# Attention values over 64 weight columns with two heads side by side, a new split of the convolution taps, and four early output blocks in a two-layer encoder

## The chip, the cores and the metric

The kernel runs on one core of one Trainium2 chip. The metric is the device time of one execution in microseconds (us). Where the profile speaks of engines, PE is TensorE's matmul side, PEld its weight loads, DVE is VectorE, ACT is ScalarE, POOL is GpSimd and SP is SyncE, which issues most DMAs.

## The reference

Two layers of a Conformer-like block work on 512 tokens of 1024 features in float32. Each layer is a half-weighted SwiGLU, a mixing part, a second SwiGLU and a norm. The change lies in the mixing part alone, which runs two groups beside each other on the same projection: attention in 8 heads (queries and keys of 96 features, values of 64, block-causal by chunks of 64 tokens), and a causal depthwise convolution of 31 taps over 512 channels, with layer norm and swish. One projection takes both:

```python
h = rms_norm(x, mix_norm[l])
p = h @ w_in[l]
attn = mla_group(p[..., :o_kv], p[..., o_kv:o_pe], p[..., o_pe:o_cv], ...)
conv = conv_group(p[..., o_cv:], conv_w[l], conv_b[l], conv_ln_g[l], conv_ln_b[l])
x = x + jnp.concatenate([attn, conv], axis=-1) @ w_out[l]
...
probs = jax.nn.softmax(scores, axis=-1).astype(vs.dtype)
outs.append(jnp.einsum('bhqk,bhkd->bqhd', probs, vs))
...
y = lax.conv_general_dilated(u, conv_w[:, None, :], window_strides=(1,), padding=[(CONV_K - 1, 0)], ...)
return jax.nn.silu(layer_norm(y + conv_b, ln_g, ln_b))
```

## The kernel before, in words

Features lie on the 128 partitions and the 512 tokens along the free axis. Weight products are made from operands split into a high and a low part, three matmuls each (`mm3`, L154 to L156), with 512, 384, 288 or 256 moving columns. The products inside attention are plain float32 matmuls, and each of those stands as two instructions (each with its own weight load) in the trace.

`mix_body` first makes the projections in the order of `SEQ`: convolution group 0, the query latents, the gate of group 0, group 1, the key latents, the queries (`queries`), the keys (`keys`), then groups 2 and 3. In `queries` and `keys` each of the four token tiles ends in a power of -1/2 on POOL (`rsqrt`, L173), called `scq` for queries and `sck` for keys; DVE multiplies the keys by `sck` (L782 to L785), and only then does PE turn queries and keys of the first two heads (L811, L816).

Then the heads run staggered by `ORDER`: `turn` (transposes), `scores` (four blocks of 128 to 512 columns, L834, with the mask L835; DVE takes the maximum, L836; ACT the exponential, L840), `turn_p` (10 transposes of the probabilities, L855, copied by DVE and ACT, L858), `values` and `turn_out`. In `values` the turned probabilities are the 128 weight columns and 64 columns of V move, 10 matmuls a head (L868). When a pair of heads is done, DVE multiplies by the reciprocal sums (L875), PE turns the result back (L886), and `split` makes its high and low part (ACT L161, DVE L162).

The convolution has four groups of 128 channels and 31 taps, `CONV = "DAAD"`. In a group of kind D, DVE runs 30 multiply-adds into a PSUM bank (L922). In a group of kind A, ACT makes each tap's product into one of three `pr` buffers (L926) and POOL adds it (L930); from the 16th tap on, and in all of group 2 and later, those adds are issued behind the last `sck`. The four groups are summed by POOL (`ysum`, L944 to L946), PE takes the mean over channels (L948), DVE subtracts it (L954), ACT squares, PE sums the squares (L198), POOL takes the root, PE spreads it (L217), and scaling, swish and `split` (L964, L966, L161, L162) give the convolution half of the output projection. `early_groups` issues the attention half of the first output blocks (12 matmuls each) into that chain of small steps: `WOG = 3` blocks, two between L948 and L198, one between L198 and L217.

The scheduler fixes the order on each engine when the program is built, from program order, dependences, and `issue_after`, which holds an instruction behind another. Each engine then runs its list strictly in order.

Of the kernel before, what the change touches and what calls it, by code (L numbers as in the profile page):

```python
# [7 lines left out]
FP = mybir.dt.float32  # L8
# [4 lines left out]
ALU = mybir.AluOpType  # L13
# [61 lines left out]
def encoder_kernel(ctx: ExitStack, tc: tile.TileContext, xT, consts, vecs, rgain, wgu1, wd1, wdq1,  # L75
# [11 lines left out]
    def nm(s):  # L87
        uid[0] += 1
        return f"{s}{uid[0]}"
# [527 lines left out]
    def mix_body(kpool, l, gx, norm, done):  # L617
        u, order = [], {}

        def kept(dt=FP):  # L620
            return kpool.tile([P, S], dt, tag="m", name=nm("m"), bufs=2 * WIDE)
        ys = [None if kind == "D" else kpool.tile([P, S], FP, tag="y", name=nm("y"), bufs=2) for kind in CONV]

        def glu(pa, pg):
            tg = tmp()
# [40 lines left out]
        def latent_k():  # L666

            pk = [bank() for _ in range(NT)]
            for k0 in range(0, KD, 3):
                n = min(3, KD - k0)  # L670
                wh, wl = load_w(wkl[l, :, k0 * KW:(k0 + n) * KW], n * KW, "k")
                for k in range(k0, k0 + n):
                    cs = slice((k - k0) * KW, (k - k0 + 1) * KW)
                    for t in range(NT):
                        ts_ = slice(t * P, (t + 1) * P)
                        mm3(pk[t][:, :KW], gx[k][0][:, ts_], gx[k][1][:, ts_], wh[:, cs], wl[:, cs],
                            k == 0, k == KD - 1)
            for t in range(NT):
                A.copy(ckl[t // 2][:, t % 2], pk[t][:, :KVL])
                A.copy(cke[:, t], pk[t][:, KVL:KW])  # L680
                j = tmp()
                A.activation(j[:, :KVL], pk[t][:, :KVL], AF.Square, accum_out=ssl[:, t:t + 1])
                j = tmp()
                A.activation(j[:, :DR], pk[t][:, KVL:KW], AF.Square, accum_out=sspe[:, t:t + 1])


        tabs = []
# [173 lines left out]
        def values(h):  # L861

            if h % 2 == 0:
                heads[h]["po"] = bank()
            po = heads[h - h % 2]["po"].rearrange("p (t h d) -> p t h d", t=NT, h=2)
            for t in range(NT):
                for j in range(t + 1):
                    T.matmul(po[:, t, h % 2], heads[h]["pt"][j][:, (t - j) * P:(t - j + 1) * P],  # L868
                             vs[j][:, h * DV:(h + 1) * DV], start=j == 0, stop=j == t)
# [5 lines left out]
            V.tensor_tensor(o.rearrange("p (t h d) -> p t h d", t=NT, h=2), po,  # L875
                            rs[:, :, :, None].to_broadcast([P, NT, 2, DV]), ALU.mult)
            heads[h]["o"] = o

        def turn_out(h):

            if h % 2 == 0:
                return
            o = heads[h]["o"]
            ps = bank()
            for t in range(NT):
                T.transpose(ps[:, t * P:(t + 1) * P], o[:, t * P:(t + 1) * P], ident)  # L886
# [27 lines left out]
        for c in range(4):  # L914
            kind = CONV[c]
            acc = psum.tile([P, S], FP, tag="cv", name=nm("cv"), bufs=1) if kind == "D" else ys[c]
            tap = lambda k: cw[:, c * CK + k:c * CK + k + 1]
            A.activation(acc, u[c], AF.Identity, scale=tap(CK - 1), bias=cb[:, c:c + 1])  # L918
            for k in range(CK - 2, -1, -1):
                s = CK - 1 - k  # L920
                if kind == "D":
                    V.scalar_tensor_tensor(acc[:, s:], u[c][:, :S - s], tap(k), acc[:, s:], ALU.mult, ALU.add)  # L922
                    continue
                pr = kpool.tile([P, S], FP, tag="pr", name=nm("pr"), bufs=3)
                if kind == "A":
                    A.activation(pr[:, s:], u[c][:, :S - s], AF.Copy, scale=tap(k))  # L926
                else:
                    G.tensor_scalar(pr[:, s:], u[c][:, :S - s], tap(k), None, ALU.mult)
                with tc.issue_after(order["keys"]) if s >= PAUSE or c > 1 else nullcontext():
                    order["conv"] = G.tensor_tensor(acc[:, s:], acc[:, s:], pr[:, s:], ALU.add).ins  # L930
            if kind == "D":
                A.copy(u[c], acc)
                ys[c] = u[c]
        early = []

        def early_groups(ms):
# [11 lines left out]
        T.matmul(pm, onesm, ysum, start=True, stop=True)  # L948
        if PRELOAD:
# [291 lines left out]
```

## Time and profile before

| | us |
|---|---|
| three runs, median (lowest to highest) | 1799.76 (1798.87 to 1799.94) |
| the profiled execution | 1798.87 |
| its span, first to last instruction | 1797.1 |
| PE busy in the span | 1781.8 (99%) |
| DVE busy | 1494.5 (83%) |
| ACT busy | 1107.5 (62%) |
| POOL busy | 421.5 (23%) |

The span is divided into stages with different limits. The mixing part stands at about 350 to 560 us in layer 0 and 1240 to 1450 us in layer 1. POOL has almost all its work there. The granted TensorE clock is full in the whole execution. PE's ends are modelled, so a group of matmuls is best timed by its start and the start of what follows it.

### The profile page before, as it was taken

The page shows a single profiled execution, that of the slowest core. Times are in us where ns is not written, and L with a number is a line of the kernel's source. Part 1 is how long each engine was busy: PE and PEld are TensorE (multiplying, and loading weights), DVE is VectorE, ACT ScalarE, POOL GpSimd, SP SyncE. Part 2 cuts the span into 40 slices and gives each one's busy share as a digit, 9 for nine tenths or more (in the row PEclk, how much of TensorE's full clock was granted, in tenths as well). Part 3 has the DMA queues.
Part 4 walks back from the last instruction along what each step waited for, and adds up shares of the span by engine and source line. Part 5 has one row for each costly group of instructions (what it writes and reads, how often), then busy time and mean ns, then how long its engine had stood idle before and what let it go on. Part 6 is the DMA issues. An engine that isn't in the chain of part 4 may idle for free.

```text
span 1797.1 us, 29235 instructions
## 1 busy us (share of the span) xinstructions
PE 1781.8 (99%) x11334; PEld 1602.4 (89%) x11334; DVE 1494.5 (83%) x2299; ACT 1107.5 (62%) x1721; POOL 421.5 (23%) x343
## 2 busy tenths in 40 slices
PE   9999999999999999999999999999999999999998
PEld 7899999888788899999888999998978788999997
DVE  7898988589956989898779989876998668989883
ACT  5575756457953575756645757554779435756564
POOL 1000000258943000000310000002689410000002
PEclk9999999999999999999999999999999999999999
DMA  5657575325103466665426575743250125575742
GB/s 168 171 131 182 135 177 123 109 88 134 33 22 102 123 164 161 155 160 132 123 65 170 122 194 122 193 112 111 81 147 7 46 82 160 140 183 134 182 117 74
DMA packets 70413, 226.16 MB, mean 126 GB/s; under 512 B 7937, under 2 KB 8321, under 8 KB 70273
## 3 DMA queue, kind: packets, MB, share of 16 engines
q1 hardware_dynamic: 54000, 169.74, 30.3%
q0 software_dynamic: 16128, 54.53, 18.0%
q8 instruction: 89, 1.46, 0.3%
q14 instruction: 52, 0.42, 0.1%
q10 hardware_dynamic: 144, 0.00, 0.0%
HBM read 222.15 MB, written 2.10 MB: 125 GB/s over the span
## 4 chain that ended last, share of the span: by engine, by line
PE 91%; ACT 3%; DVE 2%; POOL 2%; issue 1%; DMA 0%; SPq 0%; ACTq 0%; POOLq 0%; DVEq 0%
PE ps L154 24%; PE ps L156 23%; PE ps L155 23%; PE ps L373 11%; PE ps L374 6%; PE ps L868 1%; PE ps L834 1%; POOL y L930 1%; ACT pr L926 1%; ACT r L840 1%; PE ps L855 1%; PE ps L198 0%; POOL sck L173 0%; PE ps L217 0%; DVE wl L246 0%
## 5 line engine op out<-in xcount | busy, mean ns | idle before, releaser
L155 PE MATMUL ps<-r,wh 128*128 128x256 f32 (+1 forms) x2540 | 806.8, 318 | 0.0
L154 PE MATMUL ps<-r,wh 128*128 128x256 f32 (+1 forms) x2540 | 803.6, 320 | 2.2 <-ACT wh L138 0.7
L156 PE MATMUL ps<-r,wl 128*128 128x256 f32 (+1 forms) x2348 | 749.2, 321 | 0.0
L154 PEld LDWEIGHTS ps<-r,wh 128*128 128x128 f32 x2540 | 480.5, 189 | 47.0 <-ACT wh L138 3.6
L155 PEld LDWEIGHTS ps<-r,wh 128*128 128x128 f32 x2540 | 481.6, 190 | 35.8 <-DVE r L162 1.5
L156 PEld LDWEIGHTS ps<-r,wl 128*128 128x128 f32 x2348 | 445.1, 190 | 33.5 <-DVE wl L144 0.4
L373 PE MATMUL ps<-xj,wh 128*128 128x512 f32 x864 | 303.9, 392 | 0.0
L138 ACT CAST wh<-raw 128x1024 fp32r<-128x1024 f32 (+3 forms) x148 | 131.9, 899 | 208.1 <-PE ps L155 125.8
L390 POOL DMA_DIRECT2D ls<-in_wgu x72 | 62.7, 871 | 734.7 <-ACT ls L389 595.3
L244 ACT CAST wh<-fr 128x1024 fp32r<-128x1024 f32 (+1 forms) x160 | 157.6, 985 | 104.4 <-DVE fr L410 53.2
L144 DVE TENSOR_TENSOR wl<-raw,wh 128x1024 fp32r<-128x1024 f32 (+3 forms) x132 | 145.3, 1108 | 91.3 <-ACT wh L138 90.9
L246 DVE TENSOR_TENSOR wl<-fr,wh 128x1024 fp32r<-128x1024 f32 (+1 forms) x160 | 182.3, 1139 | 20.3 <-ACT wh L244 20.3
L373 PEld LDWEIGHTS ps<-xj,wh 128*128 128x128 f32 x864 | 161.4, 188 | 30.1
L930 POOL TENSOR_TENSOR y<-y,pr 128x511 f32<-128x511 f32 (+14 forms) x120 | 158.6, 1322 | 54.5 <-ACT pr L926 47.1
L374 PE MATMUL ps<-xj,ls 128*128 128x256 f32 x576 | 161.3, 280 | 0.0
L244 ACT CAST wh<-raw 128x1024 fp32r<-128x1024 f32 (+1 forms) x100 | 98.2, 982 | 45.1 <-PE ps L155 24.2
L246 DVE TENSOR_TENSOR wl<-raw,wh 128x1024 fp32r<-128x1024 f32 (+1 forms) x100 | 113.5, 1135 | 14.2 <-ACT wh L244 13.7
L191 POOL TENSOR_TENSOR r<-r,t 128x512 f32<-128x512 f32 x45 | 75.0, 1676 | 175.6 <-ACT t L187 174.8
L374 PEld LDWEIGHTS ps<-xj,ls 128*128 128x128 f32 x576 | 108.3, 188 | 0.0
L389 ACT ACTIVATE ls<-fr 128x1024 fp32r<-128x1024 f32 (+1 forms) x56 | 56.1, 1002 | 74.5 <-PE ps L374 42.8
L926 ACT ACTIVATE pr<-m,vec 128x511 f32<-128x511 f32 (+14 forms) x120 | 85.7, 736 | 13.2 <-POOL y L930 13.2
L922 DVE SCALAR_TENSOR_TENSOR cv<-m,vec,cv 128x511 f32<-128x511 f32 (+14 forms) x120 | 87.8, 732 | 3.6 <-ACT cv L918 2.2
(241 smaller groups left out, 2944.9 us busy)
## 6 DMA issues: line engine op xcount, KB each, us to landing
fr<-in_wgu SPq DMA_DIRECT2D x112, 512.0 KB, 4.2
ls<-in_wgu POOLq DMA_DIRECT2D x72, 512.0 KB, 6.2
raw<-in_wgu SPq DMA_DIRECT2D x62, 512.0 KB, 4.5
fr<-in_wdq SPq DMA_DIRECT2D x48, 384.0 KB, 4.6
ls<-in_wdq POOLq DMA_DIRECT2D x32, 384.0 KB, 4.8
raw<-in_wd SPq DMA_DIRECT2D x32, 384.0 KB, 3.2
raw<-in_wd SPq DMA_DIRECT2D x32, 256.0 KB, 2.8
raw<-in_wcv SPq DMA_DIRECT2D x16, 512.0 KB, 3.6
```

Source lines behind the costliest of these rows:

```text
L138: order["cast"] = A.copy(hi[:, :w], raw[:, :w]).ins
L144: (G if kind in POOLW.split() else V).tensor_tensor(lo[:, :w], raw[:, :w], hi[:, :w].bitcast(FP), ALU.subtract)
L154: T.matmul(o, lh, rh, start=first, stop=False, skip_group_check=free)
L155: T.matmul(o, lh, rl, start=False, stop=False, skip_group_check=free)
L156: order["mm"] = T.matmul(o, ll, rh, start=False, stop=last, skip_group_check=free).ins
L244: A.copy(hi[:, :w], src[:, :w])
L246: order["lo"] = V.tensor_tensor(lo[:, :w], src[:, :w], hi[:, :w].bitcast(FP), ALU.subtract).ins
L373: T.matmul(o, w[0][:, c], both, start=start and k == 0, stop=False, skip_group_check=True)
L374: last = T.matmul(o[:, 0:HS], w[1][:, c], both[:, 0:HS], start=False, stop=k == 3, skip_group_check=True).ins
L922: V.scalar_tensor_tensor(acc[:, s:], u[c][:, :S - s], tap(k), acc[:, s:], ALU.mult, ALU.add)
L926: A.activation(pr[:, s:], u[c][:, :S - s], AF.Copy, scale=tap(k))
L930: order["conv"] = G.tensor_tensor(acc[:, s:], acc[:, s:], pr[:, s:], ALU.add).ins
```

## The change

Three things are altered, all in `mix_body`, and so twice in the program.

**Values.** For a pair of heads, V's 64 columns are the weights and the turned probabilities move (128 to 512 columns, 4 matmuls a head). The first head of a pair writes PSUM partitions 0 to 63, the second 64 to 127, in turns; each instruction carries a tile of 128 rows by 64 columns, at column 0 or 64. The result comes out already turned, so the four transposes of `turn_out` go. The reciprocal sums must now run along the free axis: 8 matmuls a pair spread them (a broadcast column as weights, the identity moving), and ACT copies the result to SBUF. DVE's multiplication reads that copy, and `split` reads SBUF instead of PSUM.

**Convolution.** `TAPS = (14, 20, 31, 0)` gives each group the number of taps that go by ACT and POOL; DVE makes the rest in PSUM and adds the two sums. Group 2 is all ACT and POOL, group 3 all DVE. From the fifth tap on, ACT's products of groups 1 and 2 are held behind the last square of the key latents. `ysum` is built by DVE as the groups end.

**Output.** `WOG = 4` and `E1 = 1`: one block's attention half is issued ahead of the mean, one between mean and squares, one between squares and spread, one behind.

```diff
-CONV = "DAAD"
+TAPS = (14, 20, 31, 0)
+HELD = 5
...
-E1 = 0
-YP = 1
+E1 = 1
 E2 = 2
 E3 = 3
-WOG = 3
+WOG = 4
...
-            return kpool.tile([P, S], dt, tag="m", name=nm("m"), bufs=2 * WIDE)
+            return kpool.tile([P, S], dt, tag="m", name=nm("m"), bufs=10)
...
         def values(h):
             if h % 2 == 0:
-                heads[h]["po"] = bank()
-            po = heads[h - h % 2]["po"].rearrange("p (t h d) -> p t h d", t=NT, h=2)
-            for t in range(NT):
-                for j in range(t + 1):
-                    T.matmul(po[:, t, h % 2], heads[h]["pt"][j][:, (t - j) * P:(t - j + 1) * P],
-                             vs[j][:, h * DV:(h + 1) * DV], start=j == 0, stop=j == t)
-            if h % 2 == 0:
                 return
             rs = small.tile([P, NT, 2], FP, tag="rs", name=nm("rs"))
             V.reciprocal(rs, heads[h - 1]["sums"])
+            pr = bank()
+            for t in range(NT):
+                for i in range(2):
+                    T.matmul(pr[i * DV:(i + 1) * DV, t * P:(t + 1) * P], rs[:, t, i:i + 1].to_broadcast([P, DV]),
+                             ident, start=True, stop=True)
+            r = tmp()
+            A.copy(r, pr)
+            po = bank()
+            for j in range(NT):
+                for i in range(2):
+                    T.matmul(po[i * DV:(i + 1) * DV, j * P:], vs[j][:, (h - 1 + i) * DV:(h + i) * DV],
+                             heads[h - 1 + i]["pt"][j], start=j == 0, stop=j == NT - 1)
             o = tmp()
-            V.tensor_tensor(o.rearrange("p (t h d) -> p t h d", t=NT, h=2), po,
-                            rs[:, :, :, None].to_broadcast([P, NT, 2, DV]), ALU.mult)
+            V.tensor_tensor(o, po, r, ALU.mult)
             heads[h]["o"] = o
...
-            o = heads[h]["o"]
-            ps = bank()
-            for t in range(NT):
-                T.transpose(ps[:, t * P:(t + 1) * P], o[:, t * P:(t + 1) * P], ident)
-            at.append(split(ps, kept if len(at) < 2 else slot))
+            at.append(split(heads[h]["o"], kept if len(at) < 1 else slot))
...
+        ysum = None
+        for c, n in enumerate(TAPS):
             tap = lambda k: cw[:, c * CK + k:c * CK + k + 1]
...
+            if n:
+                A.activation(ys[c], u[c], **first)
+            for s in range(n or 1, CK):
+                k = CK - 1 - s
+                if s == n:
+                    A.activation(acc[:, s:], u[c][:, :S - s], AF.Copy, scale=tap(k))
                     continue
+                if s == 1 and not n:
+                    A.activation(acc, u[c], **first)
+                V.scalar_tensor_tensor(acc[:, s:], u[c][:, :S - s], tap(k), acc[:, s:], ALU.mult, ALU.add)
+            for s in range(1, n):
+                k = CK - 1 - s
                 pr = kpool.tile([P, S], FP, tag="pr", name=nm("pr"), bufs=3)
-                if kind == "A":
+                with tc.issue_after(order["latent"]) if c and s >= HELD else nullcontext():
                     A.activation(pr[:, s:], u[c][:, :S - s], AF.Copy, scale=tap(k))
-                else:
-                    G.tensor_scalar(pr[:, s:], u[c][:, :S - s], tap(k), None, ALU.mult)
                 with tc.issue_after(order["keys"]) if s >= PAUSE or c > 1 else nullcontext():
-                    order["conv"] = G.tensor_tensor(acc[:, s:], acc[:, s:], pr[:, s:], ALU.add).ins
-            if kind == "D":
+                    order["conv"] = G.tensor_tensor(ys[c][:, s:], ys[c][:, s:], pr[:, s:], ALU.add).ins
+            if not n:
                 A.copy(u[c], acc)
                 ys[c] = u[c]
+            elif n < CK:
+                V.tensor_tensor(ys[c][:, n:], ys[c][:, n:], acc[:, n:], ALU.add)
+            if c:
+                last, ysum = ysum or ys[0], u[1]
+                V.tensor_tensor(ysum, last, ys[c] if n else acc, ALU.add)
...
-        ysum = tmp()
-        G.tensor_tensor(ysum, ys[0], ys[1], ALU.add)
-        G.tensor_tensor(ysum, ysum, ys[2], ALU.add)
-        (G if YP else V).tensor_tensor(ysum, ysum, ys[3], ALU.add)
```

Three places of the order tell what the lists became. The first is PE in layer 0, from the last transposes of head 1 on; in the kernel before:

```order
L855 MATMUL ps_4946<-cst,r_4820 128x128
L855 MATMUL ps_4946<-cst,r_4821 128x128
L868 MATMUL ps_4951<-m_4748,r_4877 128x64 x2
L868 MATMUL ps_4951<-m_4757,r_4884 128x64
L868 MATMUL ps_4951<-m_4748,r_4877 128x64
L868 MATMUL ps_4951<-m_4757,r_4884 128x64
L868 MATMUL ps_4951<-m_4766,r_4891 128x64
```

In the changed kernel, at the end of the first pair (L871 spreads the reciprocals, L878 makes the values, L835 is a score block):

```order
L871 MATMUL ps_5011<-cst,rs_5009 64x128 x8
L835 MATMUL ps_4966<-r_4908,r_4901 128x256
L836 LDWEIGHTS mrow
L836 MATMUL ps_4966<-mneg,mrow 128x64
L878 MATMUL ps_5022<-r_4878,m_4749 64x512
L878 MATMUL ps_5022<-r_4934,m_4749 64x512
L878 MATMUL ps_5022<-r_4885,m_4758 64x384
L878 MATMUL ps_5022<-r_4941,m_4758 64x384
L878 MATMUL ps_5022<-r_4892,m_4767 64x256
L878 MATMUL ps_5022<-r_4948,m_4767 64x256
L878 MATMUL ps_5022<-r_4885,m_4776 64x128
L878 MATMUL ps_5022<-r_4941,m_4776 64x128
```

The two heads' matmuls stand in turns and both wait for the pair's second head. The second place is POOL in layer 0, from the root of the key latents on; before, between the first `scq` and the last `sck` there is no add of the convolution:

```order
L173 TENSOR_TENSOR scq_4370<-ssh_3860,minus_half 128x8
L173 TENSOR_TENSOR scq_4401<-ssh_3860,minus_half 128x8
L173 TENSOR_TENSOR scq_4442<-ssh_3860,minus_half 128x8
L691 TENSOR_TENSOR tab_13382<-cst,rg 128x64 x4
L173 TENSOR_TENSOR scq_4473<-ssh_3860,minus_half 128x8
L173 TENSOR_TENSOR sck_4503<-ssk_3861,minus_half 128x8
L173 TENSOR_TENSOR sck_4521<-ssk_3861,minus_half 128x8
```

In the changed kernel (L936 is the add), from the second `scq` to the third `sck`:

```order
L173 TENSOR_TENSOR scq_4402<-ssh_3861,minus_half 128x8
L936 TENSOR_TENSOR y_3847<-y_3847,pr_5441 128x502
L173 TENSOR_TENSOR scq_4443<-ssh_3861,minus_half 128x8
L936 TENSOR_TENSOR y_3847<-y_3847,pr_5444 128x501
L936 TENSOR_TENSOR y_3847<-y_3847,pr_5447 128x500
L692 TENSOR_TENSOR tab_13365<-cst,rg 128x64 x4
L936 TENSOR_TENSOR y_3847<-y_3847,pr_5450 128x499
L173 TENSOR_TENSOR scq_4474<-ssh_3861,minus_half 128x8
L936 TENSOR_TENSOR y_3847<-y_3847,pr_5453 128x498
L173 TENSOR_TENSOR sck_4504<-ssk_3862,minus_half 128x8
L173 TENSOR_TENSOR sck_4522<-ssk_3862,minus_half 128x8
L936 TENSOR_TENSOR y_3847<-y_3847,pr_5456 128x497
```

Two more adds stand between the first `scq` and the second, and three instead of two between the root of the key latents and the first `scq`: 11 adds where there were 2. The third place is DVE where the convolution of layer 0 ends, just behind the last tap of group 3, in the changed kernel (L944 is the sum over groups, L881 the values' multiplication, L859 a copy of turned probabilities, L961 the subtraction of the mean):

```order
L944 TENSOR_TENSOR m_4057<-m_4057,cv_5565 128x512
L881 TENSOR_TENSOR t_5261<-ps_5252,t_5250 128x512
L859 COPY r_5264<-ps_5263 128x512
L859 COPY r_5278<-ps_5277 128x256
L162 TENSOR_TENSOR r_5283<-t_5261,r_5282 128x512
L961 TENSOR_TENSOR y_3846<-y_3846,ps_5612 128x512
L961 TENSOR_TENSOR y_3847<-y_3847,ps_5612 128x512
L961 TENSOR_TENSOR y_3848<-y_3848,ps_5612 128x512
L961 TENSOR_TENSOR m_4702<-m_4702,ps_5612 128x512
L881 TENSOR_TENSOR t_5308<-ps_5299,t_5297 128x512
L162 TENSOR_TENSOR r_5311<-t_5308,r_5310 128x512
L191 TENSOR_TENSOR r_5630<-r_5630,t_5633 128x512
```

The mean, which stood behind the whole of attention, now stands ahead of the last pair's multiplication on DVE, and on PE ahead of 7 of its 8 value matmuls and behind 6 matmuls of the first output block.

More of the change, by code (lines that the diff above doesn't have):

```diff
@@ L620, in kept @@
         def kept(dt=FP):
[L621 to L622 removed]
+            return kpool.tile([P, S], dt, tag="m", name=nm("m"), bufs=10)
+        ys = [kpool.tile([P, S], FP, tag="y", name=nm("y"), bufs=3) if n else None for n in TAPS]
         def glu(pa, pg):
@@ L913, in mix_body @@
         cw, cb = vv(l, "cw"), vv(l, "cb")
[L914 to L916 removed]
+        ysum = None
+        for c, n in enumerate(TAPS):
             tap = lambda k: cw[:, c * CK + k:c * CK + k + 1]
[L918 to L923 removed]
+            acc = psum.tile([P, S], FP, tag="cv", name=nm("cv"), bufs=1) if n < CK else None
+            first = dict(func=AF.Identity, scale=tap(CK - 1), bias=cb[:, c:c + 1])
+            if n:
[4 more added lines that the diff above has]
+                    A.activation(acc[:, s:], u[c][:, :S - s], AF.Copy, scale=tap(k))
+                    continue
+                if s == 1 and not n:
[3 more added lines that the diff above has]
+                k = CK - 1 - s
```

4 lines of the change are left out of this document (2 added, 2 removed).

## The prediction

> **What bounds the kernel now.** I read the page's first part, then busy time by stage, then PE's waits, then single instructions.
>
> ```profile
> PE 1781.8 (99%) x11334; PEld 1602.4 (89%) x11334; DVE 1494.5 (83%) x2299; ACT 1107.5 (62%) x1721; POOL 421.5 (23%) x343
> ```
>
> PE is the bound of the whole. The stages of the mixing part (columns: stage, then busy time and instructions of PE, PEld, DVE, ACT, POOL) show where it has company:
>
> ```profile
> 320.00:449.70 129.70, 129.68 (x648) 111.63 (x647) 104.12 (x159) 79.67 (x141) 69.58 (x51) 1.00 0.40 112
> 449.70:507.60 57.90, 55.20 (x402) 45.09 (x401) 50.56 (x98) 50.78 (x122) 52.40 (x43) 1.00 0.11 24
> 507.60:560.00 52.40, 52.07 (x227) 41.54 (x226) 35.07 (x39) 26.90 (x39) 23.04 (x11) 1.00 0.26 79
> 1339.60:1397.30 57.70, 55.13 (x402) 44.92 (x400) 49.65 (x96) 51.19 (x124) 53.07 (x44) 1.00 0.11 23
> ```
>
> Projections and output run at PE's pace. In the attention stage (second and fourth row) PE idles 2.7 us, but DVE, ACT and POOL are each busy over 50 of 57.9 us: whoever shortens PE there soon meets another engine. Work shifted on the other engines in the first and third row costs nothing as long as PE's operands still come in time. PE's waits in layer 0:
>
> ```profile
> PE ps L834 <- ACT r L840: 1.5, 3, 0.7
> PE ps L886 <- DVE t L875: 0.8, 1, 0.8
> ```
>
> **Values on PE.** Durations go from start to next start.
>
> ```profile
> 467.18 2.31 PEld L868 LDWEIGHTS ps<-m,r 128*128 128x128 f32 x20
> 467.19 2.44 PE L868 MATMUL ps<-m,r 128*128 128x64 f32 x20
> 469.47 0.65 PE L834 MATMUL ps<-r,r 96*128 96x256 f32 x2
> 469.95 0.19 PE L835 MATMUL ps<-mneg,mrow 128*128 128x64 bf16 x1
> 471.27 0.39 PE L834 MATMUL ps<-r,r 96*128 96x128 f32 x2
> 471.49 0.20 PE L835 MATMUL ps<-mneg,mrow 128*128 128x64 bf16 x1
> 471.53 0.89 PE L834 MATMUL ps<-r,r 96*128 96x384 f32 x2
> 472.25 0.19 PE L835 MATMUL ps<-mneg,mrow 128*128 128x64 bf16 x1
> 472.29 1.10 PE L834 MATMUL ps<-r,r 96*128 96x512 f32 x2
> 473.22 0.20 PE L835 MATMUL ps<-mneg,mrow 128*128 128x64 bf16 x1
> 506.91 0.66 PE L886 MATMUL ps<-cst,t 128*128 128x128 f32 x4 [0.78 <-DVE t L875]
> 507.40 1.02 PE L948 MATMUL ps<-t,onesm 128*128 128x512 f32 x2
> ```
>
> A head's 20 value instructions take 469.47 - 467.19 = 2.28 us, as long as their weight loads (2.31): the loads of 128 columns set the pace, not the 64 moving ones. Removed per layer: 8 x 2.28 = 18.2, and 16 transposes, 4 in 0.49, = 2.0; together **20.2 us**. Added: a float32 matmul takes 0.93, 0.72, 0.48 and 0.22 us for 512, 384, 256 and 128 moving columns (L834 to L835), so a head takes 2.35 and 8 heads 18.8; the spread is 32 matmuls of 128 columns, 32 x 0.22 = 7.0. One behind the other that is 25.8, a **loss of 5.6 us**. If the two halves of the array run together it is 12.9, a **gain of 7.3 us**. No instruction of 64 weight columns stands in the trace, so these are the ends. I take the full overlap: the lists alternate between the halves, neighbours share no weights and no output partitions, and nothing in a row makes one half wait for the other.
>
> The Trainium skill ("TensorEngine Tiling (Array Packing)", Key Properties) has tiles load and multiply in parallel, but says that a change of tiling mode drains TensorE; no row before shows either. The last matmul of a run ends 0.16 us after the next starts (467.19 + 2.44 against 469.47); 14 changes a layer at that price, an estimate, are 2.2 us, which would use up PE's slack found below and leave the sum as it is.
>
> **Which engine then ends the stage.** The marker is the mean, L948, at 507.40 in layer 0. *By PE:* scores start here,
>
> ```profile
> 449.68 0.38 PE L834 MATMUL ps<-r,r 96*128 96x128 f32 x2
> ```
>
> and 57.7 us later comes L948. Less 2.7 idle, less 7.3, less 1.9 for seven value matmuls now behind L948, plus 6 x 0.23 for those of the early block now ahead: 449.7 + 47.2 = 496.9. *By DVE:*
>
> ```profile
> 380.71 0.69 DVE L632 TENSOR_TENSOR m<-t,t 128x512 f32<-128x512 f32 x1
> 446.44 2.37 DVE L632 TENSOR_TENSOR m<-t,t 128x512 f32<-128x512 f32 x1 [1.18 <-ACT t L628]
> 493.98 0.71 DVE L922 SCALAR_TENSOR_TENSOR cv<-m,vec,cv 128x482 f32<-128x482 f32 x1
> 494.60 1.01 DVE L858 COPY r<-ps 128x512 f32<-128x512 f32 x2
> ```
>
> DVE's last tap is through at 494.6, after 44 us without a gap, and the changed list has the same 30 taps there. Ahead of the last tap it gains a merge and two sums of 0.6 us each (spacing), of which the 1.18 us idle before L632 at 446.44 covers all but 0.7. Three instructions now read two SBUF operands while POOL adds: a sum and the `split` of one pair for certain, a second `split` at the edge. L632 shows what that costs: 0.69 with POOL quiet, 2.37 with a POOL add, so 0 to 1.7 each; I take 1.8 in all. That gives 497.1. Behind the last tap stand a `split` (0.6), two copies (0.95), a reciprocal (0.1) and the last sum (0.6): L948 at 499.4. DVE is 2.5 us later than PE and sets it. POOL does not: 34 adds against 45 stand behind the last `sck`, and the three sums have left it.
>
> **What delays the start.** Nine more adds are queued among the eight roots on POOL (11 against 2), and the last key factor releases the transposes of head 0.
>
> ```profile
> L173 POOL TENSOR_TENSOR scq<-ssh,minus_half 128x8 f32<-128x8 f32 x4 | 9.7, 2430 | 6.0 <-DVE ssh L750 5.9
> L173 POOL TENSOR_TENSOR sck<-ssk,minus_half 128x8 f32<-128x8 f32 x4 | 9.2, 2318 | 0.0
> L173 POOL TENSOR_TENSOR scq<-ssh,minus_half 128x8 f32<-128x8 f32 x4 | 10.8, 2703 | 8.0 <-DVE ssh L750 8.0
> L930 POOL TENSOR_TENSOR y<-y,pr 128x496 f32<-128x496 f32 (+29 forms) x45 | 57.3, 1274 | 5.5 <-ACT pr L926 2.6
> 440.51 1.86 DVE L785 TENSOR_TENSOR kn<-cke,scp 128x256 f32<-128x256 f32 x1
> 442.89 0.60 PE L816 MATMUL ps<-cst,kn 128*96 128x128 f32 x4
> ```
>
> The rows are the roots of layer 0, those of layer 1 (`scq`), the adds, and the end of the keys: ready at 442.4, wanted from 442.9, so there is no slack to speak of. Nine adds of 1.3 us are 11.8 us; POOL idles 6.0 among the roots of layer 0 and 8.0 in layer 1. The delay is at most 5.8 and 3.8 us. At least it is nothing: the eight roots take 18.9 us, and 8 x 1.64 (the shortest) would be 13.1, so 5.8 of them is stretch that may fall elsewhere. I take **3 us** in each layer, the middle, nearer layer 1's row. It moves the whole stage: behind PE's transposes stand the values of V, then the scores, and DVE and ACT wait for those. So L948 comes at 502.4 and PE could reach it at 499.9.
>
> **From the mean to the convolution half.**
>
> ```profile
> 506.17 0.69 DVE L875 TENSOR_TENSOR t<-ps,rs 128x512 f32<-128x512 f32 x1 [0.87 <-PE ps L868]
> 507.61 0.59 ACT L161 CAST r<-ps 128x512 fp32r<-128x512 f32 x1 [3.03 <-PE ps L886]
> 508.22 0.69 DVE L162 TENSOR_TENSOR r<-ps,r 128x512 fp32r<-128x512 f32 x1 [1.37 <-ACT r L161]
> 514.65 0.47 PE L154 MATMUL ps<-m,wh 128*128 128x512 f32 x1
> 517.52 1.02 PE L217 MATMUL ps<-t,ones 128*128 128x512 f32 x2
> 521.45 1.20 PE L154 MATMUL ps<-r,wh 128*128 128x512 f32 x4
> ```
>
> Before, 14.05 us pass from L948 (507.40) to the first matmul on the convolution half (521.45). Now the last pair's multiplication, cast and `split` (0.69 + 0.59 + 0.69 = 2.0) stand in DVE's queue between the mean's subtraction and the squares: 16.0. PE's own work in that time fits: rest of the values 1.9, 42 matmuls at 2.87 / 12 = 0.24 (514.65 to 517.52) are 10.1, small sums and spread about 2.2. So 502.4 + 16.0 = 518.4 against 521.45: **3.0 us earlier** a layer. From there PE's rows are the same: before, too, a fourth block was under way between L217 and 521.45, so four early blocks cost and bring nothing by themselves.
>
> **Edits at nothing.** Until 442 us PE runs without a gap (first row of the stages) and the other engines' changes there (26 taps and a merge for 30 on DVE; POOL beginning when group 0 is ready and not group 1) hide behind it; if a weight cast came late behind a product that waits for POOL, each such wait would cost its length. The four copies of the spread on ACT (0.6 each) are paid by 11 products fewer (about 0.6 each) behind the first exponential. Fewer buffers for kept tiles, and banks held for a shorter time, cost nothing I can see.
>
> **Sum.** 2 x 3.0 = 6.0 off the profiled execution's 1798.87 gives 1792.9; the median of the runs is 0.9 higher, so **1793.8 us**.
>
> **Rivals.** *No delay at POOL:* 2 x 6.0 off, 1787.8. For it: the stretch; against: no slack at 442.9. *Full delay:* 5.8 and 3.8 instead of 3 and 3 brings 3.6 back, 1797.4, no change that can be told: about 0.2% (3.6 us) is what a measurement of this kernel can tell. *The halves don't overlap* (slower): values and spread take 25.8 instead of 12.9. PE decides as soon as they take over 12.9 + 2.5 = 15.4. In full, L948 comes at 499.9 + 11.0 = 510.9 (1.9 of the 12.9 lies behind it), and PE's work behind it grows to 16.2: 527.1, that is 5.7 later a layer, 11.4 in all: 1811.2. For it: no row shows two halves at once, and float32 moves each column more than once (0.93 us for 512 against 0.24 for the split products); against: nothing else in the rows. The Trainium skill ("TensorE: Matmul & The Clock Gate", Measured speedup vs the span model) has 2.38x for three column tiles; by that, two give an estimated 1.59x, 16.2 us, 0.8 over the point of decision, and the time would be 1795.4.
>
> **How the numbers follow.** Forecast 0.48, own range 1790 to 1798; no delay 0.20; full delay 0.10; no overlap 0.22. Faster by over 0.2% (below 1796.2): three quarters of the forecast's and all of no delay, 0.56. Slower (above 1803.4): the no-overlap case and what a worse delay leaves, 0.24. Same: 0.20. For 8 in 10 the range goes from 1785 to 1812: it takes in no delay and no overlap as worked out, and leaves out what lies beyond them.
>
> **What would show it.** L878's pairs of 512 columns should start some 0.9 us apart per pair (overlap) or 1.9 (none). The last `sck` should end 0 to 6 us later than now and PE should wait at the transposes of the keys by as much. L948 should be released by DVE's last sum some 5 us earlier than now, the first matmul on the convolution half 3 us earlier. I am wrong if PE waits for exponentials (ACT's products held up by POOL), if casts come late before 442 us, or if POOL's last add holds DVE's second sum.

## The result, and the profile after

The change makes the kernel **slower**: 1819.12 us median of 4 runs (1818.77 to 1821.11) against 1799.51 of the kernel before beside it. The ratio is 1.0112, with a 95% interval of 1.0094 to 1.0129. The forecast was 1793.8. The profiled execution has a span of 1817.0 us (1797.1 before). Lines of the changed kernel stand one lower up to L867; the values are L871 (spread) and L878, the mean L955.

The page's first part, and PE's waits in the whole execution (us in total, times, longest):

```profile
PE 1783.2 (98%) x11238; PEld 1585.1 (87%) x11238; DVE 1517.5 (84%) x2301; ACT 1119.4 (62%) x1735; POOL 419.1 (23%) x341
```

```profile
PE ps L817 <- DVE kn L786: 15.3, 3, 7.1
PE ps L156 <- DVE wl L144: 4.5, 2, 2.5
```

PE issues 96 matmuls fewer and is busy 1.4 us longer, and two waits that were next to nothing before take 19.8 us: for the last key product, and for a weight's low part. Rows of PE in layer 0 (start, us, then the operation; a wait stands in brackets):

```profile
446.26 0.49 PE L817 MATMUL ps<-cst,kn 128*96 128x128 f32 x3
453.80 0.45 PE L817 MATMUL ps<-cst,kn 128*96 128x128 f32 x1 [7.05 <-DVE kn L786]
...
462.19 0.39 PE L835 MATMUL ps<-r,r 96*128 96x128 f32 x2
...
485.09 2.37 PE L878 MATMUL ps<-r,m 128*64 128x512 f32 x16
487.40 0.64 PE L812 MATMUL ps<-cst,q 128*96 128x128 f32 x4
...
513.47 1.02 PE L955 MATMUL ps<-m,onesm 128*128 128x512 f32 x2
...
529.01 1.21 PE L154 MATMUL ps<-r,wh 128*128 128x512 f32 x4 [0.31 <-ACT r L161]
```

The first score comes at 462.19 (449.68 before), 12.5 us later; the mean at 513.47 (507.40), 6.1 later; the convolution half at 529.01 (521.45), 7.6 later. So the stage from first score to mean did get shorter, from 57.7 to 51.3 us, and lost twice as much ahead of it. Stages, with the granted clock in the third column from the right:

```profile
414.00:424.00 10.00, 8.02 (x36) 6.39 (x35) 10.00 (x15) 9.60 (x18) 9.70 (x7) 0.99 0.01 2
424.00:428.00 4.00, 4.00 (x13) 3.14 (x12) 4.00 (x6) 2.91 (x5) 2.89 (x3) 0.61 0.79 258
428.00:445.80 17.80, 17.80 (x80) 14.66 (x79) 17.14 (x29) 8.68 (x12) 17.80 (x14) 1.00 0.38 119
451.00:458.00 7.00, 4.20 (x15) 3.66 (x16) 6.50 (x7) 6.26 (x10) 4.75 (x6) 0.51 1.00 254
462.20:513.50 51.30, 49.92 (x346) 33.49 (x345) 49.06 (x97) 45.44 (x113) 31.38 (x26) 1.00 0.10 21
1348.70:1359.00 10.30, 5.46 (x18) 4.63 (x19) 9.80 (x8) 6.24 (x10) 6.39 (x6) 0.50 0.70 156
```

Before, the clock was 1.0 there throughout. Now it halves after the wait for L144 (second row) and after the one for the key product (fourth row; sixth in layer 1), and PE's work behind each wait takes twice as long for a while. Who makes PE wait is seen on DVE and POOL, which work at the same place:

```profile
444.41 1.49 DVE L786 TENSOR_TENSOR kn<-cke,scp 128x256 f32<-128x256 f32 x1
445.83 1.96 DVE L783 TENSOR_SCALAR scp<-sck,ratio 128x8 f32<-128x8 f32 x1
...
448.30 5.45 DVE L786 TENSOR_TENSOR kn<-cke,scp 128x256 f32<-128x256 f32 x1
...
456.67 0.65 DVE L941 TENSOR_TENSOR y<-y,cv 128x492 f32<-128x492 f32 x1
...
461.71 0.74 DVE L929 SCALAR_TENSOR_TENSOR cv<-m,vec,cv 128x511 f32<-128x511 f32 x1
...
506.04 0.72 DVE L929 SCALAR_TENSOR_TENSOR cv<-m,vec,cv 128x482 f32<-128x482 f32 x1
...
508.31 0.64 DVE L944 TENSOR_TENSOR m<-m,cv 128x512 f32<-128x512 f32 x1
```

```profile
440.62 3.77 POOL L173 TENSOR_TENSOR sck<-ssk,minus_half 128x8 f32<-128x8 f32 x2
...
448.15 5.30 POOL L936 TENSOR_TENSOR y<-y,pr 128x494 f32<-128x494 f32 x4
```

The last `sck` ends at 444.4 (437.8 before, by the end of the `sck` rows). DVE's last key product then takes 5.45 us, as long as POOL's run of four adds beside it (448.15 to 453.45); with no add beside it, such a product takes 0.42 (437.99 in the kernel before). The taps of group 3 begin at 461.71, behind the merge of group 1 (456.67); the last one begins at 506.04 and ends at 506.8.

### The profile page after: what moved, and what is told of

The parts are those of the page before. It is cut to its first block, busy times and chain, and to the rows that moved or that the text cites. A ratio compares the mean times of both kernels' runs of the same rounds, so it can differ in the third digit from the quotient of the medians.

```text
span 1817.0 us, 29076 instructions
## 1 busy us (share of the span) xinstructions
PE 1783.2 (98%) x11238; PEld 1585.1 (87%) x11238; DVE 1517.5 (84%) x2301; ACT 1119.4 (62%) x1735; POOL 419.1 (23%) x341
## 5 line engine op out<-in xcount | busy, mean ns | idle before, releaser
L156 PE MATMUL ps<-r,wl 128*128 128x256 f32 (+1 forms) x2364 | 757.3, 322 | 4.7 <-DVE wl L144 4.5
L156 PEld LDWEIGHTS ps<-r,wl 128*128 128x128 f32 x2364 | 449.0, 190 | 40.2 <-DVE wl L144 6.1
L144 DVE TENSOR_TENSOR wl<-raw,wh 128x1024 fp32r<-128x1024 f32 (+3 forms) x132 | 145.4, 1110 | 89.4 <-ACT wh L138 88.3
L936 POOL TENSOR_TENSOR y<-y,pr 128x511 f32<-128x511 f32 (+23 forms) x124 | 170.6, 1393 | 38.6 <-ACT pr L934 32.8
L934 ACT ACTIVATE pr<-m,vec 128x511 f32<-128x511 f32 (+23 forms) x124 | 89.1, 740 | 27.0 <-POOL y L936 26.6
L390 POOL DMA_DIRECT2D ls<-in_wdq x32 | 27.7, 865 | 262.1 <-ACT ls L389 262.1
```

The source lines that it names most:

```text
L144: (G if kind in POOLW.split() else V).tensor_tensor(lo[:, :w], raw[:, :w], hi[:, :w].bitcast(FP), ALU.subtract)
L156: order["mm"] = T.matmul(o, ll, rh, start=False, stop=last, skip_group_check=free).ins
L390: G.dma_start(out=lo[:, :n], in_=w, accum_op=ALU.add)
L936: order["conv"] = G.tensor_tensor(ys[c][:, s:], ys[c][:, s:], pr[:, s:], ALU.add).ins
```

## The experiments

The theory from this: POOL's adds among the roots delay the keys, through POOL's own queue and through DVE's starved instructions, and the halved clock makes the wait dearer. The rivals: the new values cost the time; the early block does; the clock alone does. A second cause came up on the way, the late taps of group 3. Ratios are to the kernel before on the same chip, with a 95% interval; times are medians.

| run | us | ratio |
|---|---|---|
| values_only | 1807.55 | 1.0044 (1.0029 to 1.0059) |
| old_values | 1828.60 | 1.0164 (1.0149 to 1.0179) |
| adds_held | 1804.95 | 1.0028 (1.0017 to 1.0040) |
| adds_behind_kn | 1816.81 | 1.0095 (1.0079 to 1.0112) |
| evac | 1811.38 | 1.0066 (1.0052 to 1.0080) |
| held_evac | 1800.78 | 1.0007 (0.9998 to 1.0016) |
| held_evac15 | 1803.76 | 1.0023 (1.0014 to 1.0032) |
| held_evac_old | 1802.91 | 1.0020 (1.0012 to 1.0029) |
| held_evac_h12 | 1805.64 | 1.0034 (1.0021 to 1.0046) |
| held_evac_h12_e0 | 1801.55 | 1.0010 (1.0001 to 1.0019) |
| held_evac_e0 | 1794.48 | 0.9973 (0.9962 to 0.9984) |
| held_evac_e0w3 | 1794.78 | 0.9976 (0.9966 to 0.9986) |
| held_evac_h8_e0 | 1808.51 | 1.0047 (1.0033 to 1.0061) |
| best17 | 1805.94 | 1.0041 (1.0029 to 1.0054) |
| e0_old | 1798.12 | 0.9998 (0.9989 to 1.0007) |
| late_early | 1817.66 | 1.0101 (1.0087 to 1.0115) |
| pe_warm | 1830.04 | 1.0171 (1.0158 to 1.0185) |
| one_half | 1832.51 | 1.0186 (1.0172 to 1.0200) |

### The values alone, and everything but the values

`values_only` is the kernel before with the new `values` and `turn_out`; `old_values` is the changed kernel with the old ones. The core of the edit (the other way round for `old_values`):

```
-                    T.matmul(po[:, t, h % 2], heads[h]["pt"][j][:, (t - j) * P:(t - j + 1) * P],
-                             vs[j][:, h * DV:(h + 1) * DV], start=j == 0, stop=j == t)
+                    T.matmul(po[i * DV:(i + 1) * DV, j * P:], vs[j][:, (h - 1 + i) * DV:(h + i) * DV],
+                             heads[h - 1 + i]["pt"][j], start=j == 0, stop=j == NT - 1)
```

> The kernel before with only the new values (64 weight columns, two heads at once); taps, POOL's list and early blocks as before. Theory (the loss of 12.5 us a layer ahead of the first score comes from POOL's adds among the roots, the wait for the last key factor and the halved clock behind it): the last sck ends at 437.8 as before, PE waits under 1 us at the key transposes, the granted clock stays at 1.0, and the time is 1790 to 1802, since POOL's own sums still set the mean. Rival (the new values cost the time: mode changes, more matmuls): 1810 or more, with the attention stage longer than 57.7 us.

> The changed kernel with the values of before (128 weight columns, one head after the other); taps, POOL's list and early blocks as changed. Theory: PE waits 7 to 8 us a layer at the key transposes as in the changed kernel, and the attention stage is 4 to 6 us longer than its 51.3, so 1825 to 1832, slower than the changed kernel. Rival (the new values cost the time): back to 1800 to 1806.

PE's longest waits with the new values alone, in the whole execution:

```profile
PE ps L948 <- POOL t L946: 11.0, 2, 6.2
PE ps L834 <- ACT r L840: 3.3, 8, 0.7
```

No wait at the key transposes, as the theory has it. But the time lies between the two expectations: POOL's sums still set the mean (507.88, before 507.40), what PE saved became a wait of 4.9 us for them, and behind the wait the clock is 0.56 for 3.5 us:

```profile
508.00:511.50 3.50, 3.50 (x7) 2.13 (x8) 1.51 (x3) 0.82 (x3) 0.00 (x0) 0.56 0.00 0
```

So shorter values alone lose, in this schedule: in the main, PE becomes idle and then slow. By the ratios the second run is 9.4 us slower than the changed kernel: the values are no cause of its loss, as the theory said.

### Where the adds stand

```
-                with tc.issue_after(order["keys"]) if s >= PAUSE or c > 1 else nullcontext():
+                with tc.issue_after(order["keys"]) if s >= PAUSE or c and s >= HELD else nullcontext():
```

> The changed kernel with POOL's adds of group 1 from the fifth tap on queued behind the eight roots instead of among them. Theory: the last sck ends at 438 to 439, the wait at the key transposes goes from 7.1 to under 2 us, the clock stays at 1.0 there, and the time is 1794 to 1804; what could hold it there is POOL, whose adds then end some 8 us later than 498.5. Rival (DVE's last key product is held up by the adds whatever their place): that product still takes over 4 us and the time is over 1810. Rival (early blocks, mean, or values cost the time): 1812 or more.

Both waits are gone (neither L817 on L786 nor L156 on DVE's L144 is in the list), the first score is back at 449.7 and 15 us of the 20 are recovered. The time is just above the upper end of what was expected, and POOL is not what holds it: its last add ends at 504.7, DVE's last sum follows only at 510.0, since DVE's taps of group 3 begin at

```profile
466.19 0.74 DVE L929 SCALAR_TENSOR_TENSOR cv<-m,vec,cv 128x511 f32<-128x511 f32 x1
```

15.5 us later than in the kernel before (450.70). That is the second cause, below.

The other half of the theory, DVE's starvation, by itself: adds among the roots stay, all others wait for the last key product.

```
+            with tc.issue_after(order["keys"]):
+                order["kn"] = G.tensor_scalar(tiny("mk", 1), kn[:, NT - 1, H - 1, DQ - 1:DQ], 1.0, None, ALU.mult).ins
...
-                with tc.issue_after(order["keys"]) if s >= PAUSE or c > 1 else nullcontext():
+                with tc.issue_after(order["kn"]) if s >= PAUSE or c > 1 else nullcontext():
```

> The changed kernel with its adds among the roots left where they are, but all others held until the last key product of DVE is done (one POOL instruction on one column that reads the product stands ahead of them). Theory (half of the wait is DVE's last product, 5.45 us beside POOL adds that run back to back): the product takes about 0.5 us, the wait at the key transposes falls from 7.1 to 2 to 3 us, the clock may fall or not, and the time is 1806 to 1812. Rival (the late root is all): the product may be short but the wait stays above 5 us and the time above 1814.

```profile
446.04 0.41 DVE L786 TENSOR_TENSOR kn<-cke,scp 128x256 f32<-128x256 f32 x1
```

(DVE's last key product in layer 0.) It takes 0.41 instead of 5.45 and the wait at the key transposes is gone altogether, more than expected: the starved product made the 7 us wait, and the late root hides behind PE's own lateness (L144). The time hardly follows (ratio 1.0095 against 1.0112, intervals overlap). In layer 0 the first score comes at 453.59, 8.6 us earlier than in the changed kernel, but the mean at 513.84 (513.47): an earlier start alone brings nothing there. The stall moved, and the edit itself has a part in it: the held adds are those that group 1's merge needs, and DVE's queue stands until they are done.

```profile
454.11 0.67 DVE L943 TENSOR_TENSOR y<-y,cv 128x492 f32<-128x492 f32 x1 [4.95 <-POOL y L938]
```

PE then waits for ACT and DVE, the clock is 0.50 from 460 to 467, and the taps of group 3 start at 459.2. Neither theory had that. So this run shows what the wait was made of, and not what it cost. PE's longest waits now (L814 are query transposes, L837 scores):

```profile
PE ps L156 <- DVE wl L144: 4.4, 2, 2.5
PE ps L814 <- DVE m L903: 2.0, 1, 2.0
PE ps L837 <- ACT r L816: 1.9, 1, 1.9
```

### Group 3 behind group 1's merge

All groups that DVE has taps of accumulate in one PSUM bank (`cv`, one buffer). Group 1's merge on DVE frees it, and the merge waits for POOL's adds on group 1. So group 3, which before could start at once, now waits for POOL. The edit copies the accumulator with ACT to the idle tile `u[0]`; `evac` has it alone, `held_evac` with the adds held.

```
+                part = acc
+                if c:
+                    part = u[0]
+                    A.copy(part[:, n:], acc[:, n:])
-                V.tensor_tensor(ys[c][:, n:], ys[c][:, n:], acc[:, n:], ALU.add)
+                V.tensor_tensor(ys[c][:, n:], ys[c][:, n:], part[:, n:], ALU.add)
```

> The kernel with the adds held, and group 1's accumulator copied by ACT from its PSUM bank to the idle tile of group 0 right after its own taps, so that the bank is free for group 3 at once (the merge then reads the copy). Theory (in the changed kernel the 30 taps of group 3 cannot begin before the merge of group 1, which waits for POOL's adds on group 1; DVE therefore ends its taps at 506 to 508 instead of 494.6): taps of group 3 begin by 450 instead of behind 461, the last one ends at 495 to 500, POOL's last add at 505 becomes the bound, the mean stands at 503 to 507, and the time is 1790 to 1798. Rival (the sum of DVE's work ends late wherever the taps stand): last tap still after 505, time 1802 to 1806.

> The changed kernel with only the accumulator copied; adds stay among the roots. Theory (both causes are there, and either alone would hold the mean at 511 to 513): taps of group 3 begin some 5 us earlier, the wait at the key transposes and the halved clock stay, and the time is 1812 to 1819. Rival (the taps of group 3 were the only cause): 1806 or less.

First and last rows of DVE's taps in `held_evac`, then its last sum, and the mean on PE:

```profile
450.41 0.76 DVE L929 SCALAR_TENSOR_TENSOR cv<-m,vec,cv 128x511 f32<-128x511 f32 x1 [0.98 <-ACT cv L928]
...
499.15 0.71 DVE L929 SCALAR_TENSOR_TENSOR cv<-m,vec,cv 128x482 f32<-128x482 f32 x1
...
504.45 0.69 DVE L948 TENSOR_TENSOR m<-m,cv 128x512 f32<-128x512 f32 x1
```

```profile
507.21 1.02 PE L959 MATMUL ps<-m,onesm 128*128 128x512 f32 x2
```

Taps start 16 us and end 8 to 9 us earlier than with the adds held alone, and the time is that of the kernel before; it is 3 us above the expected range, because the mean does not follow DVE's last sum (through at 505.1) for 2.1 us. `evac` alone brings 8 us, a little more than expected, but not as expected: taps of group 3 begin only 2.2 us earlier (459.53), while POOL's adds now run in pairs beside DVE's key products (two of these take 3.22 us together), so the wait at the key transposes fell as well. It is no test of the accumulator alone.

### The early block ahead of the mean

`held_evac_e0` has only the first line of this beside `held_evac`; `held_evac_e0w3` and `late_early` (the changed kernel) have both.

```
-E1 = 1
+E1 = 0
...
-WOG = 4
+WOG = 3
```

> The kernel with adds held and the accumulator copied (1800.8 us), with the mean's matmul ahead of the first early block (E1 = 0; four early blocks). Theory (DVE's last sum is through at 505.1, but on PE the mean stands behind the block's six products and the last pair's values, and starts at 507.2): the mean comes 1 to 3 us earlier a layer, the time is 1794 to 1798. Rival (the softmax of the last head ends the stage, and PE's order only shuffles it): 1799 to 1802.

> The same with three early blocks, as before the change (WOG = 3). Theory (PE has enough to do behind the mean with three blocks too, the rest follows later either way): within 1.5 us of the kernel with four. Rival (the fourth block fills the wait for the variance and the spread): 2 to 5 us above it.

> The changed kernel with the mean ahead of the early blocks and three of them, as before (E1 = 0, WOG = 3). Theory (the stage starts late and DVE ends its sums at 509; PE brings the mean 4.5 us later at 513.5 because of what stands ahead of it): the mean comes 1 to 4 us earlier a layer, 1811 to 1817. Rival (the early block is what the changed kernel loses): 1806 or less. Rival (it costs nothing): 1818 to 1820.

The mean on PE in `held_evac_e0`:

```profile
505.57 1.10 PE L959 MATMUL ps<-m,onesm 128*128 128x512 f32 x2 [1.38 <-DVE m L948]
```

Now the mean comes right behind DVE's last sum. 1794.48 us beats both kernels (0.9973, whole interval below 1): it is the version to keep. The fourth block makes no difference (0.9973 and 0.9976). In the changed kernel itself the edit does little: `late_early` falls between its two expectations and its interval overlaps the changed kernel's (1.0101 against 1.0112); there PE comes to the mean at 512.37 without waiting for it, 3 us behind DVE's last sum (through at 509.3).

What the values are worth when nothing is late, with the old ones put back (the edit of `old_values`) in `held_evac` and in `held_evac_e0`:

> The kernel with adds held and the accumulator copied (1800.8 us), with the values of before. It says what the new values are worth once nothing is late. Theory (they take 6 to 7 us a layer off PE, of which a part was idle time in the stage): 1806 to 1815, with the attention stage 60 to 63 us. Rival (PE does not bound the stage at all, ACT and POOL do): 1799 to 1803.

> The kernel with adds held, accumulator copied and the mean ahead of the early blocks (1794.5 us), with the values of before. Theory (with the new values PE waits 1.4 us a layer for DVE's last sum, so it has that much slack; the old ones take 6 to 7 us more on PE, of which 2 to 4 fill idle time): 1800 to 1806. Rival (the new values are worth nothing, other engines bound the stage): 1793 to 1797.

With the mean in front the new values bring 0.9998 - 0.9973 = 0.0025, 4.5 us in two layers; with the block in front, 0.0013, where the intervals overlap. Both runs lie below what the theory expected: I had priced the old values too high. In `e0_old` the mean of layer 0 stands at 507.01, 1.4 us later than in `held_evac_e0` (505.57), so most of the 6 to 7 us that they take on PE fell where PE waits anyway.

### Moving more work ahead of the roots

Two ways to take adds off the end of the stage: both holds begin later, or fewer taps of group 1 go to ACT and POOL.

```
-HELD = 5
+HELD = 12
...
-TAPS = (14, 20, 31, 0)
+TAPS = (14, 15, 31, 0)
```

`held_evac_h12` and `held_evac15` have one of these each beside `held_evac`; `held_evac_h12_e0`, `held_evac_h8_e0` (8 instead of 12) and `best17` (17 instead of 15) have one beside `held_evac_e0`.

> The kernel with adds held and the accumulator copied, but the fifth to eleventh tap of group 1 are multiplied and added early, before the eight roots (both holds begin at the twelfth tap). Theory (with the delays gone the stage is bound by ACT and POOL, which do 45 products and adds behind the roots, not by PE): seven products and adds fewer there bring POOL's last add from 503 to 494, the last exponentials and with them the last pair of values 2 to 5 us earlier, and the time to 1788 to 1796. Rival (work moved ahead of the roots holds up casts or roots there as in the changed kernel): a PE wait before 450 and 1799 or more.

> The same, with the mean's matmul ahead of the first early block instead of behind it (E1 = 0; four early blocks stay). Theory (on PE's queue the mean waits for the block's products with the last pair): the mean is 1 to 3 us earlier a layer and the time 1 to 5 us below that of the kernel with E1 = 1. Rival (the block in front costs nothing since the sums are as late): within 1 us of it.

> The same as the kernel with E1 = 0 and four blocks, with both holds from the eighth tap on. Theory (three products and adds fewer behind the roots, and ACT's copies of the key latents not yet late): 1792 to 1797, 0 to 3 us below it, no wait at L716. Rival (ACT's copies of the key latents come late already): a PE wait at L716 of 0.5 us or more and the time above it.

> The same, with 15 instead of 20 taps of group 1 on ACT and POOL and 16 on DVE. Theory: five POOL adds (some 6.5 us) less behind the roots, five DVE taps (3.2 us) more ahead of them where DVE has room; if POOL's end sets the mean it comes 3 to 6 us earlier a layer and the time is 1784 to 1792. Rival (DVE is full ahead of the roots, weight casts come late behind the added taps, and PE waits and drops its clock): 1795 or more. Rival (PE or DVE sets the mean, POOL has slack): within 2 us of the kernel with 20.

> The same kernel of 1794.5 us with 17 instead of 20 taps of group 1 on ACT and POOL and 14 on DVE. Theory (POOL's last add at 503.5 holds DVE's last two sums): three adds fewer behind the roots bring the mean 1 to 2 us earlier, 1790 to 1793. Rival (three more DVE taps ahead of the roots make the key products late, as five did: waits of 2.9 and 2.4 us): 1795 to 1802.

All are slower than their base. With a later hold ACT copies the key latents late (`held_evac_h8_e0`, PE's longest wait in the whole execution; with 12 it is as long), and with 15 taps it is the key product again (`held_evac15`):

```profile
PE ps L716 <- ACT r L679: 4.3, 2, 2.2
```

```profile
PE ps L817 <- DVE kn L786: 5.3, 2, 2.9
```

In `best17` and `held_evac_h8_e0` the program's order also puts the mean between the first two and the other 14 instructions of the last pair's values, with early blocks behind it. DVE's multiplication of that pair then waits, and the variance's sums stand behind it (`best17`):

```profile
514.30 0.69 DVE L881 TENSOR_TENSOR t<-ps,t 128x512 f32<-128x512 f32 x1 [3.14 <-PE ps L878]
```

### The clock, and the two halves

`pe_warm` fills PE's wait with 14 idle matmuls; `one_half` runs the two heads of a pair one behind the other, in the spread and in the values (shown).

```
+            if h == 0:
+                idle = bank()
+                with tc.issue_after(order["queried"]):
+                    for _ in range(FILL):
+                        order["filled"] = T.matmul(idle[:, 0:CN], ident, cst, start=True, stop=True).ins
...
-            for j in range(NT):
-                for i in range(2):
+            for i in range(2):
+                for j in range(NT):
```

> The changed kernel with 14 idle matmuls of 256 columns (some 6.7 us) on PE between the first query transposes and the first key transposes; the wait for the key factor is filled, not shortened. Theory (the mean is set by DVE, whose taps end late, and by the wait, not by PE's pace behind it): the granted clock stays at 1.0 between 451 and 458, the 24 value products take 5.6 instead of 6.6 us, and the time gains 0 to 5 us, 1814 to 1819. Rival (the halved clock is the cost): 1809 or less.

> The changed kernel with the two heads of a pair one after the other, in the spread and in the values, so that neighbours lie in the same half of the array. Theory (neighbours in different halves overlap): the 16 value instructions of a pair take 4 to 4.7 us instead of 2.31 and the spread 2 instead of 1.02; PE, which is busy 49.9 of 51.3 us in that stage, comes 8 to 13 us later a layer, less what it waits elsewhere: 1826 to 1842. Rival (the short time of a pair is due to something else than the alternation): 1817 to 1821 and 2.3 us a pair as before.

By its time `pe_warm` says nothing on the clock's price: further waits came in (6.5 us still for the key product, 3.1 for the high part of a `split`), the clock fell to 0.76 between 451 and 458 all the same, and it is 11 us slower. A price can be read elsewhere. In layer 0 `pe_warm` and `old_values` wait 1.96 and 1.95 us for the cast L144, the changed kernel 1.98. From the end of that wait to the transposes PE takes 20.99 us in both of them, where the clock stays at 1.00, and 22.63 us in the changed kernel, where it halves: 1.6 us for one stretch of 3.4 us. In the changed kernel PE worked 3.4 and 4.0 us at half clock in layer 0, 3.1 and 5.5 in layer 1. Half of that, an estimate, is 8 us: the clock alone is at most that much of the 20 us. In `one_half` the 16 value instructions of a pair take

```profile
485.50 3.93 PE L878 MATMUL ps<-r,m 128*64 128x512 f32 x16
```

3.93 instead of 2.37 us by the same modelled end, and the kernel is 13 us slower than the changed one: the alternation makes the halves overlap.

## Why the prediction was wrong

- **Values on PE: right.** A pair takes 487.40 - 485.09 = 2.31 us, and its spread about 1.0 (a row of 16 in 1.09): 4 x 3.3 = 13.2 a layer, forecast 12.9. The no-overlap rival is refuted; `one_half` shows that it would have cost less than the 25.8 priced, since a pair with one head behind the other takes 3.9, not 4.7. By the ratio that the Trainium skill gives for three tiles ("TensorE: Matmul & The Clock Gate", Measured speedup vs the span model) I had estimated 1.59 for two; the two rows give 3.93 / 2.37 = 1.66.
- **The delay at the start: the step that failed.** "I take **3 us** in each layer", with 5.8 as the most. It was 12.5 in layer 0: 3.4 ahead of the transposes, 7.05 in the wait for the last key product, and 2.1 behind it, at the halved clock. The roots were 6.6 late, a little over the bound. What the bound left out: POOL's adds starve DVE while DVE makes what POOL's roots and PE wait for. I had the price of that from L632 (0.69 against 2.37) and used it only at the end of the attention stage, 1.8 us in all, not for the key products, which stand next to the adds that I had just moved there; and 2.37 was a stall by one or two adds, not by a run of four. The last key product was even among my rows, at 1.86 us (L785, 440.51) where 0.42 is its length without an add. `adds_behind_kn` shows the product at 0.41 and no wait for it; `adds_held` gives 15 of the 20 us back. That the place of the adds costs the time is shown by `adds_held`; how the 15 us divide between late roots and starved products is not, since `adds_behind_kn` made a new stall.
- **"Edits at nothing" ahead of 442: wrong**, through the condition that was named. The cast L144 came 2.0 to 2.5 us late, in this kernel each such wait also halved the clock, and PE reached the transposes 3.4 us later (445.83 against 442.45 by the row of L812). In layer 0 up to 457 us, DVE's L707 takes 700 ns instead of 413 and L751 870 instead of 432, beside the same adds; in `adds_held` the wait for the cast is gone.
- **The clock was not in the sum at all.** The Trainium skill ("TensorE: Matmul & The Clock Gate", Part 1) says that an idle window of about 3.4 us halves it. The trace agrees on the halving, and shows it after waits of 2.0 us, though not after every such wait (last section).
- **The mean by DVE: wrong twice.** "The changed list has the same 30 taps there": it has, but they stand behind a merge that waits for POOL (first tap 461.71, before 450.70), and the last tap ends at 506.8, not at 500.1 (497.1 and the delay of 3). `held_evac` undoes this and the delay, and its taps end at 499.9. And DVE did not set the mean in layer 0: its last sum is through at 508.95, the mean starts at 513.47, and PE comes to it without a wait. PE's stage from the first score took 51.3 us, not 47.2; 1.4 of it is idle time, and the rest of the difference was not followed up.
- **From the mean to the convolution half: right.** 529.01 - 513.47 = 15.5, forecast 16.0.
- **Four early blocks: right on their number, wrong on the order.** The fourth brings nothing, but the first one ahead of the mean holds it back: the two kernels that differ in it alone are 6 us apart.
- The forecast's size was within reach of the change: with the three places mended (the adds, the accumulator, the mean) the kernel takes 1794.5 us. That this is close to 1793.8 is chance: the sum has neither these places nor the clock.

## What to carry to other kernels

When adds move on GpSimd, look at what VectorE does beside them, not only at GpSimd's own queue: an instruction of 0.4 us took 5.45 beside four adds in a row, and PE waited for it. When a group is split between two engines, ask which buffer the merge frees and who takes it next: here one PSUM bank made 30 taps wait for another engine. And expect a new wait of 2 us on PE to cost more than 2 us: behind most of such waits here, though not behind all, the clock fell to half, and one such stretch cost another 1.6 us.

## What the runs showed of the hardware

- A VectorE instruction with two SBUF operands waited for a whole run of GpSimd adds (448.30 to 453.75 beside 448.15 to 453.45), not for the one that was under way (5.30 / 4 = 1.3 us). The Trainium skill ("SBUF — State Buffer", SBUF: two separate sides) has a lock that the first comer holds for one instruction; these rows show that the waiting engine does not get it between two adds. A `TENSOR_SCALAR` of 8 columns from SBUF to SBUF was held as well (L783, 1.96 us, otherwise 0.22).
- The clock may halve behind a PE wait of about 2 us, and the length of the wait alone does not decide it. Behind 1.98 us for L144 the changed kernel ran at 0.57 for 4 us (layer 0, from 423.2); behind 1.95 and 1.96 us for the same cast `old_values` and `pe_warm` stayed at 1.00, and `held_evac15` did even behind 2.91 us (from 446.1). `best17` ran at 0.50 from 458.3 to 468.5 behind waits of 0.7 and 1.2 us. What else decides it was not measured.
